# A transformer forward pass in float32 on one core: part of FFN-in by Strassen's scheme, FFN-out in four parts

## Chip, core and metric

The kernel runs on one core of a Trainium2 chip. The metric is the device time of one execution in microseconds (us): the median of three runs of the kernel before is 2635.81 us (2635.48 to 2645.13).

## What is computed

Two stacked blocks of a diffusion-style transformer act on 256 latent tokens (LAT) and 256 context tokens (CTX) of width 1024. The change touches three of four feed-forwards (FFN) of the first block and the modulation vectors. Each FFN normalises its input, modulates it, multiplies by `w_in` (1024 x 5632: a gate and an up half of 2816 columns each), and multiplies the gated product by `w_out` (2816 x 1024):

```
def modulate(h, shift, scale):
    return h * (1.0 + scale) + shift
def swiglu(h, w_in, w_out):
    gate, up = jnp.split(h @ w_in, 2, axis=-1)
    return (jax.nn.silu(gate) * up) @ w_out
...
m_lat = (silu_c @ w_mod[l] + b_mod[l]).reshape(Bsz, N_MOD, 1, D)
m_ctx = (silu_cc @ w_mod[l] + b_mod[l]).reshape(N_MOD, D)
x = x + 0.5 * m_lat[:, 2] * swiglu(modulate(rms_norm(x), m_lat[:, 0], m_lat[:, 1]), ffn_in[l, 0], ffn_out[l, 0])
```

`N_MOD` is 9: each `w_mod[l]` is 1024 x 9216 and gives shift, scale and gate of the three sub-layers of layer l, for the latent and for the context vector. In layer 1 the context is not used behind the mixer.

## The kernel before

Activations lie transposed, features on the 128 partitions: the residual `X` is 128 x 8 x 512, 8 blocks of features by 512 tokens, LAT first. Every product is made of three matmuls (`mm3`, L172 to L174): each float32 operand is split into a high part rounded to float32r and the rest (lo), and hi*hi, hi*lo and lo*hi are summed in PSUM. Weights are loaded by `wload`: SyncE's queue (SP) starts a DMA of 128 x 1024 into a raw tile `wr`, ScalarE (ACT) casts it to `wh` (L156), VectorE (DVE) subtracts to get `wl` (L157). In these stages each of `wr`, `wh` and `wl` has a ring of six tiles.

`ffn` runs FFN-in by units u = 0 to 21, 128 gate and 128 up columns each: two tiles of weights, 2 x 8 x 3 = 48 matmuls of 512 tokens into two banks (`ps_ff`). `hidden` applies Silu on ACT (L536) and multiplies by the up bank on DVE (L537), and splits the result into a `uh` tile, both steps on GpSimd (POOL): the high part (L420) and the rest (L421). The first three units go LAT first, then CTX (`heads`), while the modulated input becomes ready; in the first FFN of the program `opening` does them, interleaved with the first modulation vectors. FFN-in comes in two halves of 12 and 10 units, each followed by FFN-out over those units: for each block m of 8 output blocks, 12 or 10 products of 512 tokens into one bank (`ps_fo`), then `residual` on DVE adds both token halves to `X` (L517). In the second half the last four blocks are computed for LAT first, then for CTX; between the two `tail` starts the norm of the next stage (`ahead`), which so runs under the CTX products.

The modulation vectors not needed yet are computed in small steps between units (`mod_steps`, called by `tick`): for 1024 columns of `w_mod` eight 128 x 1024 tiles are loaded, and DVE accumulates tile times vector into `acc` for LAT and for CTX (L307 for the first tile, L305 for the others); one step is two tiles, four DVE instructions; four steps make 1024 columns and end in matmuls (`ps_mod`). Each FFN has up to 32 steps: the first does 28, the second 32, the third 28.

Tile's scheduler orders each engine's instructions ahead of time; at run time every engine goes through its own queue in order.

## Time and profile before

| | us |
|---|---|
| median of three runs | 2635.81 |
| the profiled execution, its own time | 2637.07 |
| span from its first to its last instruction | 2635.3 |
| PE (TensorE) busy in the span | 2511.4 (95%) |
| DVE busy | 1703.4 (65%) |
| ACT busy | 1006.6 (38%) |
| POOL busy | 668.3 (25%) |

The first FFN ends 426 us from the span's start, the second lies at about 905 to 1307, the third at 1307 to 1697. Matmul ends are modelled: a 512-token matmul is shown as 0.40 us, but the next starts 0.23 us after it; so costs of PE are read from start to start.

### The profile page before, as it was taken

The numbers are of one execution on the slowest core, as the hardware profiler recorded it, in microseconds if no ns is written. First come the engines' busy times: TensorE is split into PE (matmuls) and PEld (weight loads), VectorE is DVE, ScalarE is ACT, GpSimd is POOL, SyncE is SP. The second block draws the span as 40 slices with busy tenths as digits, with TensorE's granted clock in tenths as the row PEclk, the third lists the DMA queues.
The fourth block names the chain that finished last, engine by engine and source line by source line (L and its number), as shares of the span: only waits on it lengthen the run. The fifth ranks groups of instructions, "written<-read, shape, count | busy, mean of one in ns | idle before, by whom it ended". The sixth has DMA issues, their size and how long they took to land.

```text
span 2635.3 us, 46749 instructions
## 1 busy us (share of the span) xinstructions
PE 2511.4 (95%) x19116; PEld 2056.7 (78%) x19116; DVE 1703.4 (65%) x2753; ACT 1006.6 (38%) x1876; POOL 668.3 (25%) x669
## 2 busy tenths in 40 slices
PE   7999999998888999999999999999999999999888
PEld 5777779854776887777887777976999887578775
DVE  4968754558456578776678776487554642855885
ACT  3322224336223432222332122466434643735454
POOL 2420322023443233022242022221413120012321
PEclk9999999989899999999999999999999999999998
DMA  8767543100001556665546665242664331023412
GB/s 262 218 180 217 169 135 109 41 0 1 4 4 51 147 166 182 200 207 153 152 145 191 203 197 152 70 121 73 185 185 134 87 96 41 17 75 99 104 42 64
DMA packets 426502, 321.34 MB, mean 122 GB/s; under 512 B 16784, under 2 KB 400528, under 8 KB 426288
## 3 DMA queue, kind: packets, MB, share of 16 engines
q1 hardware_dynamic: 426288, 318.36, 41.2%
q8 instruction: 150, 2.46, 0.4%
q14 instruction: 64, 0.52, 0.1%
HBM read 317.27 MB, written 1.05 MB: 121 GB/s over the span
## 4 chain that ended last, share of the span: by engine, by line
PE 85%; DVE 8%; ACT 3%; issue 2%; DMA 2%; POOL 0%; DVEq 0%; ACTq 0%; SPq 0%; POOLq 0%
PE ps_ff L172 10%; PE ps_ff L173 10%; PE ps_ff L174 10%; PE ps_pr L172 7%; PE ps_pr L173 7%; PE ps_pr L174 7%; PE ps_fo L172 5%; PE ps_fo L173 5%; PE ps_fo L174 5%; PE ps_s L725 3%; PE ps_o L760 2%; PE ps_w L967 1%; PE ps_ptr L751 1%; PE ps_pt L173 1%; PE ps_pt L174 1%
## 5 line engine op out<-in xcount | busy, mean ns | idle before, releaser
L156 ACT CAST wh<-wr 128x1024 fp32r<-128x1024 f32 (+2 forms) x402 | 417.2, 1043 | 1007.9 <-PE ps_ff L173 407.2
L157 DVE TENSOR_TENSOR wl<-wr,wh 128x1024 fp32r<-128x1024 f32 (+2 forms) x402 | 519.6, 1296 | 402.2 <-ACT wh L156 399.7
L172 PE MATMUL ps_ff<-h,wh 128*128 128x512 f32 (+1 forms) x1232 | 451.9, 367 | 0.5 <-ACT fu L536 0.5
L173 PE MATMUL ps_ff<-h,wh 128*128 128x512 f32 (+1 forms) x1232 | 451.1, 366 | 0.0
L174 PE MATMUL ps_ff<-h,wl 128*128 128x512 f32 (+1 forms) x1232 | 450.5, 366 | 0.6 <-DVE wl L157 0.6
L420 POOL TENSOR_SCALAR uh<-fu 128x512 fp32r<-128x512 f32 (+1 forms) x88 | 169.4, 1925 | 772.9 <-DVE fu L537 772.9
L174 PE MATMUL ps_pr<-h,wl 128*128 128x256 f32 (+2 forms) x920 | 306.5, 335 | 12.3 <-DVE wl L157 12.1
L172 PE MATMUL ps_pr<-h,wh 128*128 128x256 f32 (+2 forms) x920 | 306.4, 338 | 8.9 <-ACT wh L156 6.2
L173 PE MATMUL ps_pr<-h,wh 128*128 128x256 f32 (+2 forms) x920 | 306.6, 335 | 2.0 <-POOL h L457 1.1
L305 DVE SCALAR_TENSOR_TENSOR acc<-wr,csa,acc 128x1024 f32<-128x1024 f32 x224 | 296.3, 1362 | 4.4 <-DMA wr<-in_w_mod_dram 4.4
L172 PE MATMUL ps_fo<-uh,wh 128*128 128x512 f32 (+1 forms) x824 | 278.9, 340 | 0.0
L173 PE MATMUL ps_fo<-uh,wh 128*128 128x512 f32 (+1 forms) x824 | 278.7, 339 | 0.0
L174 PE MATMUL ps_fo<-uh,wl 128*128 128x512 f32 (+1 forms) x824 | 277.7, 338 | 0.0
L172 PEld LDWEIGHTS ps_ff<-h,wh 128*128 128x128 f32 x1232 | 231.6, 188 | 51.7 <-ACT wh L156 6.7
L174 PEld LDWEIGHTS ps_ff<-h,wl 128*128 128x128 f32 x1232 | 231.6, 188 | 42.2 <-DVE wl L157 1.0
L173 PEld LDWEIGHTS ps_ff<-h,wh 128*128 128x128 f32 x1232 | 231.7, 188 | 40.5
L174 PEld LDWEIGHTS ps_pr<-h,wl 128*128 128x128 f32 x920 | 177.6, 193 | 30.3 <-DVE wl L157 14.1
L172 PEld LDWEIGHTS ps_pr<-h,wh 128*128 128x128 f32 x920 | 177.4, 195 | 30.0 <-ACT wh L156 10.1
L173 PEld LDWEIGHTS ps_pr<-h,wh 128*128 128x128 f32 x920 | 177.9, 194 | 19.8 <-POOL h L457 1.6
L172 PEld LDWEIGHTS ps_fo<-uh,wh 128*128 128x128 f32 x824 | 155.0, 188 | 26.7 <-issue 8.4
L173 PEld LDWEIGHTS ps_fo<-uh,wh 128*128 128x128 f32 x824 | 155.0, 188 | 18.7 <-issue 0.8
L174 PEld LDWEIGHTS ps_fo<-uh,wl 128*128 128x128 f32 x824 | 154.9, 188 | 18.2
(628 smaller groups left out, 4207.5 us busy)
## 6 DMA issues: line engine op xcount, KB each, us to landing
wr<-in_ffn_in_dram SPq DMA_DIRECT2D x176, 512.0 KB, 4.6
wr<-in_w_mod_dram SPq DMA_DIRECT2D x144, 512.0 KB, 4.4
wr<-in_ffn_out_dram SPq DMA_DIRECT2D x88, 512.0 KB, 4.4
wr<-in_l_w_in_dram SPq DMA_DIRECT2D x55, 512.0 KB, 3.9
wr<-in_l_w_mod_dram SPq DMA_DIRECT2D x48, 512.0 KB, 4.3
wr<-in_even_w_in_dram SPq DMA_DIRECT2D x21, 512.0 KB, 4.2
wr<-in_l_w_out_dram SPq DMA_DIRECT2D x16, 512.0 KB, 3.6
wr<-in_even_w_out_dram SPq DMA_DIRECT2D x14, 512.0 KB, 4.3
```

What stands on the lines that cost most here:

```text
L156: a = nc.scalar.copy(hi[:, : kt * n], raw)
L157: b = nc.vector.tensor_tensor(lo[:, : kt * n], raw, hi[:, : kt * n].bitcast(F32), ALU.subtract)
L172: mm(ps, a[0], b[0], start=first, stop=False)
L173: mm(ps, a[0], b[1], start=False, stop=False)
L174: self.mm = mm(ps, a[1], b[0], start=False, stop=last)
L305: nc.vector.scalar_tensor_tensor(acc[i], v, cs[:, k, i:i + 1], acc[i], ALU.mult, ALU.add)
L420: nc.gpsimd.tensor_scalar(hi, src, 1.0, None, ALU.mult)
L725: nc.tensor.matmul(s, q(h, q0s[b]), k(h), start=True, stop=True)
L751: nc.tensor.transpose(tr[:, j * 128:(j + 1) * 128], e[:, j * 128:(j + 1) * 128], self.ident)
L760: nc.tensor.matmul(o[64 * par:64 * par + 64, :nq], v(2 * m + par, j), PT[m, par][:, j, :nq], start=j == 0, stop=j == nk - 1, tile_position ...
L967: nc.tensor.matmul(out(rw, b), lhsT[rw, cl], rhs(rw, cl), start=True, stop=True, tile_position=(32 * q, 32 * q))
```

## The change

`ffn2` takes the place of `ffn` in three FFNs (layer 0 both, layer 1 the first). Of its 22 units, the even ones from u = 4 (from u = 6 in the first FFN, `early`) are done by `fast`, the others by `plain` as before. `fast` takes the gate and up tiles, each cut into two halves of the contraction, as a 2 x 2 matrix and the input, cut into two halves of the contraction and LAT and CTX, as another, and forms seven products of 12 matmuls of 256 tokens instead of eight. The sums of input blocks are made once per FFN (`whole`, `T1` to `T4`), those of weights per unit on POOL (`s1` to `s4`, in two more tiles of the `wr` ring), the sums of products on DVE in `e` and `g`. The high part of `uh` is made on ACT, not POOL. FFN-out comes after 6, 6, 6 and 4 units; its weights come in 28 loads, not 22, of the same total, and their `wl` is made on POOL, not DVE; X is updated four times, not twice. Of the last four blocks' CTX products there are now 4 units' worth behind `tail`, not 10. `mod_steps` leaves out the CTX half where it is not used (`one`), and starts with a group of two chunks in the first FFN. A step is taken after every unit from u = 4 (in the first FFN: one after u = 3, two after u = 4) and after every second block of FFN-out.

```diff
+    def wload(self, w, r0, kt, c0, n, eng=None):
         _, raw = self.wraw(w[r0:r0 + kt * 128, c0:c0 + n].rearrange("(k p) n -> p k n", p=128), kt, n)
+        return self.wsplit(raw, n, eng)
...
+    def wsplit(self, raw, n, eng=None):
+        nc, m = self.nc, raw.shape[-1]
         hi, lo = self.wtile("wh", F32R), self.wtile("wl", F32R)
-        a = nc.scalar.copy(hi[:, : kt * n], raw)
-        b = nc.vector.tensor_tensor(lo[:, : kt * n], raw, hi[:, : kt * n].bitcast(F32), ALU.subtract)
+        a = nc.scalar.copy(hi[:, :m], raw)
+        b = (eng or nc.vector).tensor_tensor(lo[:, :m], raw, hi[:, :m].bitcast(F32), ALU.subtract)
...
-        for g in range(start, (nch_all + 3) // 4):
-            nch = min(4, nch_all - 4 * g)
+        n = w.shape[1] // 512
+        at = [4 * start] + list(range(4 * start + 2 if start else 4, n, 4)) + [n]
+        for c0, c1 in zip(at, at[1:]):
+            nch = c1 - c0
...
-                acc = [self.accp.tile([128, 1024], F32, tag=f"acc{i}", name="acc", bufs=1) for i in range(2)]
+                acc = [self.accp.tile([128, 1024], F32, tag=f"acc{i}", name="acc", bufs=1) for i in range(1 if c0 // 2 + h in one else 2)]
...
-                        nc.tensor.matmul(ps[q:q + 32], self.unit[:, h], acc[i][:, c * 512:c * 512 + 512], start=h == 0, stop=2 * h + 2 == nch, tile_position=(0, q))
+                        nc.tensor.matmul(ps[q:q + 32], self.unit[:, h], acc[i % len(acc)][:, c * 512:c * 512 + 512], start=h == 0, stop=2 * h + 2 == nch, tile_position=(0, q))
...
+    def ffn2(self, l, f, name, j, segs, tail):
...
+            UH = lambda dt, nm: p.tile([128, 2, 512], dt, tag="uh", name=nm, bufs=6)
+            fu = lambda: p.tile([128, 512], F32, tag="fu", name="fu", bufs=1)
+            def keep(u):
+                uh = UH(F32R, "uh")
+                self.split(uh[:, 0], uh[:, 1], u, "a", "p")
+                hid.append(uh)
+            def hidden(ps):
+                u = fu()
+                nc.scalar.activation(u, ps[0], AF.Silu)
+                nc.vector.tensor_tensor(u, u, ps[1], ALU.mult)
+                keep(u)
...
+            block = lambda t, k, s: t[:, 4 * k:4 * k + 4, s]
+            TT = p.tile([128, 4, 2, 4, 256], F32R, name="TT")
+            def whole(k, s, eng, tag):
+                t = p.tile([128, 1024], F32, tag=tag, name="tf", bufs=6 if tag == "uh" else 1).rearrange("p (k n) -> p k n", n=256)
+                eng.tensor_tensor(t, block(hi, k, s).bitcast(F32), block(lo, k, s).bitcast(F32), ALU.add)
+                return t
+            b11, b21 = whole(0, LAT, nc.gpsimd, "uh"), whole(1, LAT, nc.gpsimd, "uh")
+            b12, b22 = whole(0, CTX, nc.vector, "acc0"), whole(1, CTX, nc.gpsimd, "acc1")
+            nc.vector.tensor_tensor(b11, b12, b11, ALU.subtract)
+            nc.gpsimd.tensor_tensor(b12, b22, b12, ALU.subtract)
+            nc.vector.tensor_tensor(b22, b22, b11, ALU.subtract)
+            nc.gpsimd.tensor_tensor(b21, b21, b22, ALU.subtract)
+            T2, T1, T3, T4 = ((TT[:, i, 0], TT[:, i, 1]) for i in range(4))
+            self.split(*T2, b22, "a", "v")
+            self.split(*T1, b11, "a", "v")
+            self.split(*T3, b12, "a", "v")
+            self.split(*T4, b21, "a", "p")
+            B11, B21, B22 = ((block(hi, k, s), block(lo, k, s)) for k, s in ((0, LAT), (1, LAT), (1, CTX)))
...
+            def fast(u):
+                G, U = (self.wraw(w_in[:, o + u * 128:o + u * 128 + 128].rearrange("(k p) n -> p k n", p=128), KD, 128)[1] for o in (0, FF))
+                a11, a12, a21, a22 = G[:, 0:512], G[:, 512:1024], U[:, 0:512], U[:, 512:1024]
+                S12, S34 = self.wtile("wr", F32), self.wtile("wr", F32)
+                s1, s2, s3, s4 = S12[:, 0:512], S12[:, 512:1024], S34[:, 0:512], S34[:, 512:1024]
+                gh, gl = self.wsplit(G, 128)
+                nc.gpsimd.tensor_tensor(s1, a21, a22, ALU.add)
+                nc.gpsimd.tensor_tensor(s2, s1, a11, ALU.subtract)
+                h12, l12 = self.wsplit(S12, 128)
+                nc.gpsimd.tensor_tensor(s3, a11, a21, ALU.subtract)
+                nc.gpsimd.tensor_tensor(s4, a12, s2, ALU.subtract)
+                h34, l34 = self.wsplit(S34, 128)
+                h22, l22 = self.wsplit(a22, 128)
+                e = p.tile([128, 2, 256], F32, tag="fe", name="fe", bufs=1)
+                g = fu()
+                sub, add, mul = ALU.subtract, ALU.add, ALU.mult
+                def product(h, l, k0, b):
+                    ps = self.psa.tile([128, 512], F32, tag="a", name="ps_ff")[:, 0:256]
+                    for k in range(4):
+                        self.mm3(ps, [h[:, k0 + k], l[:, k0 + k]], [b[0][:, k], b[1][:, k]], k == 0, k == 3)
+                    return ps
+                tt = nc.vector.tensor_tensor
+                p1 = product(gh, gl, 0, B11)
+                nc.scalar.copy(e[:, 0], p1)
+                p2 = product(gh, gl, 4, B21)
+                tt(g[:, LAT], e[:, 0], p2, add)
+                p6 = product(h12, l12, 4, T2)
+                tt(e[:, 0], e[:, 0], p6, add)
+                p5 = product(h12, l12, 0, T1)
+                nc.scalar.copy(e[:, 1], p5)
+                p7 = product(h34, l34, 0, T3)
+                tt(g[:, CTX], e[:, 0], e[:, 1], add)
+                tt(e[:, 0], e[:, 0], p7, add)
+                p3 = product(h34, l34, 4, B22)
+                tt(g[:, CTX], g[:, CTX], p3, add)
+                nc.scalar.activation(g, g, AF.Silu)
+                tt(e[:, 1], e[:, 0], e[:, 1], add)
+                p4 = product(h22, l22, 0, T4)
+                tt(e[:, 0], e[:, 0], p4, add)
+                tt(g, g, e.rearrange("p a n -> p (a n)"), mul)
+                keep(g)
+            early = (l, f) == (0, 0)
+            steps = 32
+            for part, pairs in enumerate((range(0, 3), range(3, 6), range(6, 9), range(9, 11))):
+                end = part == 3
+                if part:
+                    hid.clear()
+                u0 = pairs[0] * 2
+                for u in range(u0, u0 + 2 * len(pairs)):
+                    if len(hid) <= u - u0:
+                        (plain if u % 2 or early and u < 6 else fast)(u)
+                    if u > 3 or early and u == 3:
+                        steps -= self.tick(1 + (early and u == 4), steps)
+                nk = len(hid)
+                rest = 4 if end else 0
+                wide = 8 // nk
+                side = {}
+                def blocks(m):
+                    if m % wide == 0:
+                        side[0] = self.wload(w_out, u0 * 128, nk, m * 128, wide * 128, nc.gpsimd)
...
+                for m in range(8 - rest):
+                    b = blocks(m)
+                    product(*b, slice(0, 512))
+                    self.residual(b[1], m, name, j + 2, segs)
+                    if m % 2:
+                        steps -= self.tick(1, steps)
...
-        self.fill += [m0, self.mod_steps("1", self.i["w_mod"][1], fx),
-                      self.mod_steps("s0", self.i["l0_w_mod_2"], fs, "l0_norm"), self.mod_steps("s1", self.i["l1_w_mod_2"], fs, "l1_norm")]
+        self.fill += [m0, self.mod_steps("1", self.i["w_mod"][1], fx, one=(5, 6, 7, 8)),
+                      self.mod_steps("s0", self.i["l0_w_mod_2"], fs, "l0_norm"), self.mod_steps("s1", self.i["l1_w_mod_2"], fs, "l1_norm", one=(2,))]
...
-            self.ffn(0, 0, "0", 0, segs, 2, tail=ahead)
+            self.ffn2(0, 0, "0", 0, segs, ahead)
-            self.ffn(0, 1, "0", 6, segs, 2, tail=ahead)
+            self.ffn2(0, 1, "0", 6, segs, ahead)
         if upto == 3:
             return self.dump()
         if frm < 4:
-            self.ffn(1, 0, "1", 0, segs, 2, tail=ahead)
+            self.ffn2(1, 0, "1", 0, segs, ahead)
```

## Rows read from the trace of the kernel before

**Rows 1.** The page: busy times, and the chain that ended last by engine.

```profile
PE 2511.4 (95%) x19116; PEld 2056.7 (78%) x19116; DVE 1703.4 (65%) x2753; ACT 1006.6 (38%) x1876; POOL 668.3 (25%) x669
...
PE 85%; DVE 8%; ACT 3%; issue 2%; DMA 2%; POOL 0%; DVEq 0%; ACTq 0%; SPq 0%; POOLq 0%
```

**Rows 2.** Windows of the three FFNs: length, busy per engine, clock, DMA share, GB/s.

```profile
74.00:426.00 352.00, 349.80 (x1660) 281.53 (x1659) 246.48 (x247) 90.75 (x119) 96.80 (x60) 1.00 0.58 174
955.00:1307.00 352.00, 351.75 (x1667) 281.81 (x1665) 253.39 (x250) 84.98 (x111) 90.13 (x56) 1.00 0.60 179
1345.00:1697.00 352.00, 350.76 (x1671) 282.79 (x1669) 239.97 (x243) 86.23 (x113) 85.91 (x57) 1.00 0.56 168
```

**Rows 3.** Timeline of PE, 512 tokens: the first and last of 12 matmuls.

```profile
177.27 0.40 PE L172 MATMUL ps_ff<-h,wh 128*128 128x512 f32 x1
...
179.84 0.40 PE L174 MATMUL ps_fo<-uh,wl 128*128 128x512 f32 x1
```

**Rows 4.** Timeline of PE, 256 tokens (fourth FFN): the first and last of 36.

```profile
1959.83 0.28 PE L172 MATMUL ps_ff<-h,wh 128*128 128x256 f32 x1
...
1963.97 0.28 PE L174 MATMUL ps_ff<-h,wl 128*128 128x256 f32 x1
```

**Rows 5.** The page's costliest groups: a weight load of `ps_ff`.

```profile
L172 PEld LDWEIGHTS ps_ff<-h,wh 128*128 128x128 f32 x1232 | 231.6, 188 | 51.7 <-ACT wh L156 6.7 <-issue 3.4 <-ACT fu L536 0.9
```

**Rows 6.** Timeline of PE in the second FFN: matmuls of the modulation steps.

```profile
1197.59 1.07 PE L315 MATMUL ps_mod<-acc,unit 128*32 128x512 f32 x8
...
1203.82 0.95 PE L324 MATMUL ps_mod<-c_small,gm 128*128 128x8 f32 x8
```

**Rows 7.** DVE groups by form, 1059 to 1129 us (FFN-out): busy, mean ns.

```profile
L305 DVE SCALAR_TENSOR_TENSOR acc<-wr,csa,acc 128x1024 f32<-128x1024 f32 x27 | 33.4, 1275 | 0.0
L157 DVE TENSOR_TENSOR wl<-wr,wh 128x1024 fp32r<-128x1024 f32 x13 | 15.8, 1218 | 11.8 <-ACT wh L156 11.7
L517 DVE SCALAR_TENSOR_TENSOR X<-ps_fo,M,X 128x256 f32<-128x256 f32 x14 | 6.1, 476 | 2.6 <-PE ps_fo L174 2.6
L307 DVE TENSOR_SCALAR acc<-wr,csa 128x1024 f32<-128x1024 f32 x4 | 2.8, 750 | 0.2
```

**Rows 8.** DVE groups by form, whole run: the product in `hidden`, both widths.

```profile
L537 DVE TENSOR_TENSOR fu<-fu,ps_ff 128x512 f32<-128x512 f32 x57 | 38.8, 681 | 92.0 <-PE ps_ff L174 91.9
L537 DVE TENSOR_TENSOR fu<-fu,ps_ff 128x256 f32<-128x256 f32 x20 | 8.4, 421 | 12.5 <-PE ps_ff L174 12.5
```

**Rows 9.** Timeline of DVE in the first FFN: four in a row, then one.

```profile
113.56 4.86 DVE L305 SCALAR_TENSOR_TENSOR acc<-wr,csa,acc 128x1024 f32<-128x1024 f32 x4
...
84.36 2.34 DVE L157 TENSOR_TENSOR wl<-wr,wh 128x1024 fp32r<-128x1024 f32 x1
```

**Rows 10.** Timeline of POOL at the same place as the last.

```profile
84.33 1.29 POOL L421 TENSOR_TENSOR uh<-fu,uh 128x512 fp32r<-128x512 f32 x1
```

**Rows 11.** Timeline of DVE and of POOL in the mixer, at one time.

```profile
662.53 1.29 DVE L924 TENSOR_TENSOR GM<-ps_g,c_em_mask 128x512 f32<-128x512 f32 x2 [0.83 <-PE ps_g L921]
...
662.98 1.05 POOL L953 TENSOR_TENSOR AS<-ARw,EC 128x512 f32<-128x512 f32 x1
```

**Rows 12.** Timelines at the end of the second FFN, then a window.

```profile
1288.80 0.74 POOL L391 TENSOR_TENSOR nacc<-nacc,nsq 128x256 f32<-128x256 f32 x1 [2.81 <-ACT nsq L389]
...
1291.21 0.48 DVE L517 SCALAR_TENSOR_TENSOR X<-ps_fo,M,X 128x256 f32<-128x256 f32 x1 [3.07 <-PE ps_fo L174]
...
1300.73 2.15 DVE L449 SCALAR_TENSOR_TENSOR nt<-X,M,nacc 128x256 f32<-128x256 f32 x4
...
1308.76 0.36 PE L172 MATMUL ps_pr<-h,wh 128*128 128x256 f32 x1 [1.66 <-DVE X L517]
...
1309.00:1312.40 3.40, 3.40 (x18) 3.40 (x18) 3.40 (x5) 1.46 (x4) 2.77 (x1) 0.52 0.19 52
```

**Rows 13.** Timelines of DVE and POOL at the first turn to FFN-out.

```profile
182.06 0.68 DVE L537 TENSOR_TENSOR fu<-fu,ps_ff 128x512 f32<-128x512 f32 x1
...
185.31 1.29 POOL L421 TENSOR_TENSOR uh<-fu,uh 128x512 fp32r<-128x512 f32 x1
```

More of the change, by code (lines that the diff above doesn't have):

```diff
@@ L307, in mod_steps @@
                             a = nc.vector.tensor_scalar(acc[i], v, cs[:, k, i:i + 1], None, ALU.mult)
-                            if start and (g, h) == (start, 0):
+                            if start and (c0, h) == (at[0], 0):
                                 self.order(a, self.gate[1])
@@ L331, in mod_steps @@
                     b[:, sl].rearrange("p (c s) -> p s c", s=4), ALU.add)
-            for j in (2 * g, 2 * g + 1):
+            for j in range(c0 // 2, c1 // 2):
                 if j in fixes:
@@ L350, in tick @@
     def tick(self, n=1, left=99):
-        for _ in range(n):
+        for i in range(n):
             if not self.open and left < 8:
-                return
+                return i
             left -= 1
@@ L595, in ffn, with plain, product @@
                         left -= ticks
+                last = [blocks(m) for m in range(8 - rest, 8)]
+                for s, i in segs if rest else ():
+                    for b in last:
+                        product(*b, s)
+                        self.residual(b[1], b[0], name, j + 2, [(s, i)])
+                    if s == LAT:
+                        tail()
+            assert not self.open
+    def ffn2(self, l, f, name, j, segs, tail):
+        nc, tc = self.nc, self.tc
+        w_in, w_out = self.i["ffn_in"][l, f], self.i["ffn_out"][l, f]
+        with ExitStack() as es:
+            p = es.enter_context(tc.tile_pool(name=f"ffn{l}{f}", bufs=1))
+            mod = self.modulate(name, j)
+            self.psum(es, 6, 1, 1)
+            self.accp = p
+            hid = []
+            UH = lambda dt, nm: p.tile([128, 2, 512], dt, tag="uh", name=nm, bufs=6)
[9 more added lines that the diff above has]
+                keep(u)
+            first = []
+            done = lambda m, q: first.append(q) or len(first) % 2 or hidden(first[-2:])
+            items = [(w_in, o + u * 128, 0, done) for u in range(3) for o in (0, FF)]
+            if (l, f) == (0, 0):
+                hi, lo = self.opening(mod, items, segs)
+            else:
+                tiles = self.fetch(items)
+                hi, lo = self.modulated(mod, segs)
+                self.heads((hi, lo), tiles, segs)
+            block = lambda t, k, s: t[:, 4 * k:4 * k + 4, s]
[16 more added lines that the diff above has]
+            B11, B21, B22 = ((block(hi, k, s), block(lo, k, s)) for k, s in ((0, LAT), (1, LAT), (1, CTX)))
+            def plain(u):
+                ps = []
+                for o in (0, FF):
+                    w = self.wload(w_in, 0, KD, o + u * 128, 128)
+                    q = self.psa.tile([128, 512], F32, tag="a", name="ps_ff")
+                    for k in range(KD):
+                        self.mm3(q, [w[0][:, k], w[1][:, k]], [hi[:, k], lo[:, k]], k == 0, k == KD - 1)
+                    ps.append(q)
+                hidden(ps)
+            def fast(u):
[58 more added lines that the diff above has]
+                        side[0] = self.wload(w_out, u0 * 128, nk, m * 128, wide * 128, nc.gpsimd)
+                    c = slice(m % wide * 128, m % wide * 128 + 128)
+                    q = self.psa.tile([128, 512], F32, tag="a", name="ps_fo")
+                    return m, q, [tuple(x[:, k, c] for x in side[0]) for k in range(nk)]
+                def product(m, q, w, toks):
+                    for k in range(nk):
+                        self.mm3(q[:, toks], w[k], [hid[k][:, 0, toks], hid[k][:, 1, toks]], k == 0, k == nk - 1)
+                for m in range(8 - rest):
[4 more added lines that the diff above has]
+                        steps -= self.tick(1, steps)
```

16 lines of the change are left out of this document (7 added, 9 removed).

## The prediction

> **What bounds the kernel now.** I read the page first: TensorE (PE) is busy 95% of the span and 85% of the chain that ended last [rows 1]. Then the windows of the three FFNs that change: PE is busy for 349.8 to 351.8 of 352 us at full clock, DVE for 240 to 253, POOL for 86 to 97, ACT for 85 to 91, and the DMA engines for 0.56 to 0.60 [rows 2]. The reader is to see that in these stages only columns taken from PE give time back, and that PE has no slack in which work moved to others could be late. The profiled execution took 2637.07 us, 1.26 above the median of 2635.81; sums are made against the former, and 1.3 is taken off at the end.
>
> **What PE gains.** Twelve matmuls of 512 tokens stand 2.57 us apart from first to last, 0.2336 us each [rows 3]; 36 of 256 tokens 4.14 us, 0.1183 each [rows 4]. A plain unit costs 48 x 0.2336 = 11.2 us, a fast one 84 x 0.1183 = 9.9. There are 8 fast units in the first FFN and 9 in each of the others: 26 x 1.27 = **33 us**. FFN-out keeps its matmuls.
>
> Every matmul loads its own weights, and a load takes 0.188 us [rows 5], longer than the 0.118 step of a 256-token matmul, so the loads already run under other matmuls. The Trainium skill, page "TensorE: Matmul & The Clock Gate", Part 3, The mechanism, says that a weight load overlaps running matmuls only when its row group differs; all these use all rows. By that rule a fast unit would cost 84 x (0.118 + 0.188) = 25.7 us against 48 x (0.234 + 0.188) = 20.3, and the change would lose 26 x 5.4 = 140 us. The rows contradict it, and it gets no chance.
>
> **What DVE and POOL pay.** DVE instructions in a row overlap by 0.08 us: four L305 last 4.86 [rows 9], a step of 1.20 each against a mean of 1.275 [rows 7]. So I take 1.14 for L157, 0.40 for L517, 0.67 for L307 [rows 7], 0.60 and 0.34 for L537 at 512 and 256 tokens [rows 8], these two also for the new sums of those widths, which the trace doesn't show. Four modulation steps are 14 L305 and 2 L307, 18.1 us, 4.53 a step; half where one vector is left out.
>
> The decisive rows are those where DVE and POOL meet. An L157 that starts with POOL's L421 of 1.29 us takes 2.34 instead of 1.22: DVE stood 1.12 [rows 9, 10]. A DVE product that reads one operand from PSUM keeps its time beside a POOL instruction of two inputs, which keeps its 1.05 too [rows 11]. So two-input work from SBUF on the two engines doesn't add up side by side; it queues. A POOL instruction of 512 columns that writes float32 takes 1.05 [rows 11], one that writes float32r 1.29 [rows 10], and one of 256 columns 0.74 [rows 12]. From these I estimate 1.85 us for 768 columns, 2.4 for 1024, and 1.7 for 1024 in float32, and at 1.12/1.29 = 87% a stall of DVE of 0.91 per `s` sum, 1.12 per L421, 1.6 per `wl` of FFN-out, and 9.4 in all for the six POOL instructions of `whole` and T4.
>
> The Trainium skill, page "SBUF — State Buffer", Who interferes with whom, says that a two-input DVE instruction and a GpSimd instruction that reads SBUF exclude each other for the whole instruction. By that rule the stall is 1.29, not 1.12, and the forecast would be about 10 us later; I keep the row.
>
> Now **one pair of units** (plain and fast) with two full steps. PE: 11.2 + 9.9, and the matmuls of two steps, at most 0.4 each (eight of 1.07 in all per four steps, eight of 0.95 per eight) [rows 6]: 21.9 us. DVE from SBUF: plain 2 x 1.14; fast 3 x 1.14 + 0.60 for the half tile, 2 x 0.34 + 0.60; steps 9.1: 16.7. DVE from PSUM: 0.60 + 5 x 0.34 = 2.3. POOL's stall: 4 x 0.91 + 2 x 1.12 = 5.9. If POOL always works while DVE reads PSUM, DVE needs 22.6; if never, 24.9. Before, two units took PE 23.2 and DVE 4 x 1.14 + 1.2 + 9.1 + 2.2 = 17.1. So DVE with POOL becomes the limit, by 0.7 to 3.0 us a pair. I take 23.6, **1.7 over**: POOL's instructions are often pending when DVE turns to PSUM. With half steps DVE needs 19.1, and PE stays the limit.
>
> **FFN-out** of six units: PE 48 x 3 x 0.2336 = 33.6 and 1.6 for four steps, 35.2. DVE: 18.1 in steps, 16 x 0.40 = 6.4 for four-part residuals (PSUM), stalls of 8 x 1.6 = 12.9: 31.0 to 37.4, since moving `wl` to POOL takes 8 x 0.86 off DVE and gives 12.9 back as stall. I take 34: within PE's time.
>
> **The setup** of the input's sums is 6 x 1.14 on DVE and 9.4 of stall. In the first FFN it meets units 3 to 5 with four steps: 6.8 + 18.1 + 6.8 + 3.4 + 9.4 and 1.8 from PSUM, 44.5 to 46.3 against PE's 35.2, so 10 over. In the other two it can run under the CTX half of `heads`; I leave 2 each.
>
> Half steps are the second FFN's last twelve and the third's first four and last four; counted through, six pairs of units with full steps stand in each FFN ahead of its last part, which is light. **Excess**: first FFN 10 + 6 x 1.7 = 20; second 2 + 6 x 1.7, less 2.8 that a pair with half steps gives back, 9; third 2 + 6 x 1.7 = 12; 41 us. Against it stands DVE's lead: six `wl` tiles make one pair, so at the start of a stretch its tiles can be some 10 us ahead. That would leave 10, 0 and 2. But a part's last L537 stands at the end of what DVE has queued: at the first turn it ended at 182.7, some 4 us after FFN-in's last matmul, and L421 at 186.6 [rows 3, 13]; that cost nothing because eleven units' products, 7.7 us, come before its own in the first block of FFN-out. Now five do, 3.5 us. What DVE is behind comes out there. I take **22 us**, between 12 with the whole lead and 41 without.
>
> **The ends of the FFNs.** Between the last LAT and the end of CTX PE had 4 x 10 x 3 x 0.1183 = 14.2 us; it will have 5.7. From the last LAT residual to the first modulated tile it took 9.5 us (1291.2 to 1300.7), and PE began 8 us later, at 1308.8, and then for 3.4 us was granted 0.52 of the clock, nearly all of it the lower of its two levels, 1.2 GHz [rows 12]. The chain's own pieces (a square, two small matmuls, a root, a copy) are shorter than 5.7; what stretched it were casts, L157 and matmuls queued between. So 0 to 5.5 per FFN; I take **5** in all.
>
> **The rest at nothing.** ACT takes over the high part of `uh` and 1.5 casts per fast unit more, some 3 us of a pair, at a busy share of a quarter [rows 2]; if ACT fell behind, POOL's `s` sums would wait for nothing, but casts of the next unit would. SP issues six more loads per FFN and gives two `wr` tiles per fast unit to S12 and S34; DMA is at 0.6 [rows 2], but with a load's wait uncovered each would cost PE up to its landing. On POOL's queue `s1` to `s4` stand behind the last unit's L421, which waits for L537; behind `s4` wait the cast and L157 of the last two products. The new wait of PE is for them, covered by a whole plain unit, 11 us. Regrouping the modulation chunks changes no count.
>
> **Sum**: 2637.1 - 33 + 22 + 5 = 2631; on the median, **2630 us**.
>
> **Rivals.** First, **the lead holds**: excess at its floor of 0.7 a pair, all but 4 us absorbed, 2 us at the ends: -33 + 6, 2609. For it: PE idles 0.2 to 2.2 us in each window and DVE about 100 [rows 2], so the order of the queues leaves room. Against it: the pair's sum above uses that room up. Second, on the other side, **the shared path is the limit**: no earlier lead helps and each part's excess comes out at its turn to FFN-out: 41 us at the middle price, 81 at the upper ones (24.9 and 37.4). The ends cost 10, and at each of 12 turns half of the 2.5 us by which a chain of 6 us (4 to L537's end, a cast, L421) outlasts its 3.5 of cover, 15. That gives 2637 - 33 + 41 + 10 + 15 = 2670, without the turns 2655; I take 2662, with 2710 as the upper end. It decides from the point where DVE and POOL together need over 23 us a pair. If waits then bring PE to its lower clock [rows 12], it is more. Third, that fast units do not come to 9.9 us because products of 12 matmuls wait for banks: part of the second, no case of its own.
>
> **Chances.** Forecast 0.42 (2618 to 2648), first rival 0.26 (2604 to 2618), second 0.32 (2649 to 2710). Half a per cent, 13 us, is about what can be told from no change here. Faster than 2622.6: the first rival's 0.26 and 0.10 of the forecast's, 0.36. Slower than 2649: 0.32. Within: 0.32. For eight in ten I leave some 0.08 below 2608 and 0.1 above 2676.
>
> **What will show it.** Right: `ps_ff` at 256 tokens steps by 0.118 in these FFNs; DVE busy over 95% in the windows of FFN-in with full steps; L157 and L305 of over 2 us beside POOL's L421 and `s` sums; PE's idle time in these FFNs some 25 us, ended by DVE (`wl`, or `uh` at the turns to FFN-out), most in the first FFN. Wrong: PE busy all through (first rival), or idle over 50 us or at the lower clock (second); a wait for DMA or ACT would show that I set them to nothing wrongly.

## The result, and the profile after

The changed kernel takes 2779.91 us (2778.77 to 2781.82) against 2635.91 for the kernel before: **1.053 times as long** (95% interval 1.050 to 1.056). The forecast was 2630. The page of its profiled execution (busy times, then the chain by engine):

```profile
PE 2543.0 (92%) x19836; PEld 2107.5 (76%) x19836; DVE 1907.3 (69%) x2995; ACT 1120.8 (40%) x2076; POOL 965.5 (35%) x809
...
PE 58%; DVE 22%; issue 8%; DMA 5%; ACT 4%; POOL 3%; SPq 0%; DVEq 0%; ACTq 0%; POOLq 0%
```

Against [rows 1], DVE and POOL are busy 204 and 297 us longer and PE's share of the chain has fallen from 85% to 58%. The three feed-forwards, from the first unit behind `heads` to the last product (columns as in [rows 2]):

```profile
73.00:489.00 416.00, 363.45 (x1874) 298.25 (x1874) 324.99 (x329) 122.64 (x171) 183.81 (x99) 0.94 0.50 152
1034.00:1421.00 387.00, 356.36 (x1917) 296.26 (x1916) 317.21 (x325) 119.45 (x168) 176.64 (x96) 0.96 0.57 172
1465.00:1849.00 384.00, 355.71 (x1918) 297.30 (x1916) 302.67 (x321) 119.07 (x168) 182.96 (x97) 0.96 0.54 162
```

Read from the timeline to a tenth, these spans are 415.6, 387.1 and 383.8 us, 1186.5 together; before they were 350.2, 351.6 and 350.2, 1052.0. So 134.5 us of the loss lie inside the three FFNs and some 10 outside them. PE's matmuls should have taken 33 less: 168 us have to be explained. DVE is busy for 78 to 82% of these spans, though PE is idle in them for 28 to 52 us (length less busy time) and is granted less than the full clock. Three FFN-in stretches of six units:

```profile
166.00:262.00 96.00, 77.65 (x422) 65.78 (x421) 81.08 (x85) 26.66 (x38) 36.03 (x18) 0.89 0.57 173
297.00:386.00 89.00, 72.39 (x417) 61.15 (x417) 82.61 (x79) 23.80 (x33) 35.55 (x17) 0.94 0.61 190
1111.00:1200.00 89.00, 74.51 (x420) 63.56 (x419) 86.95 (x81) 24.65 (x34) 37.33 (x17) 0.90 0.66 202
```

The forecast's own prices give PE 65.7 us for three pairs of units. DVE is busy 84, 93 and 98% of the time: in the worst stretch it is not full. What a wait costs shows on PE's timeline in the second FFN:

```profile
1262.32 0.28 PE L176 MATMUL ps_ff<-TT,wh 128*128 128x256 f32 x1
...
1263.62 0.28 PE L178 MATMUL ps_ff<-TT,wl 128*128 128x256 f32 x1
1263.83 2.07 PE L320 MATMUL ps_mod<-acc,unit 128*32 128x512 f32 x8
1268.79 0.38 PE L176 MATMUL ps_ff<-TT,wh 128*128 128x256 f32 x1 [2.89 <-DVE fe L718]
...
1270.51 0.41 PE L177 MATMUL ps_ff<-TT,wh 128*128 128x256 f32 x1
1270.73 0.41 PE L178 MATMUL ps_ff<-TT,wl 128*128 128x256 f32 x1
1273.28 0.58 PE L176 MATMUL ps_ff<-TT,wh 128*128 128x256 f32 x1 [2.14 <-ACT fe L703]
```

The first two rows are the ends of one product: 11 steps in 1.30 us, 0.118 each, as costed [rows 4]. Then PE waits for a sum on DVE, falls to half its clock (0.22 a step; 0.50 is granted from 1271 on, 1.2 GHz) and waits again, for the copy of a first product. The third reading is ACT's timeline at one turn from a fast to a plain unit, and POOL's at the same time:

```profile
199.34 1.04 ACT L160 CAST wh<-wr 128x1024 fp32r<-128x1024 f32 x1 [1.94 <-DMA wr<-in_ffn_in_dram]
208.77 1.05 ACT L160 CAST wh<-wr 128x1024 fp32r<-128x1024 f32 x1 [8.39 <-POOL wr L685]
209.72 0.58 ACT L325 COPY gm<-ps_mod 128x512 f32<-128x512 f32 x1
210.20 0.62 ACT L422 CAST uh<-fu 128x512 fp32r<-128x512 f32 x1
...
212.67 0.60 ACT L633 ACTIVATE fu<-ps_ff 128x512 f32<-128x512 f32 x1 [1.30 <-POOL uh L427]
```

```profile
201.40 3.46 POOL L684 TENSOR_TENSOR wr<-wr 128x512 f32<-128x512 f32 x1 [13.94 <-DVE fe L718]
...
207.03 1.71 POOL L685 TENSOR_TENSOR wr<-wr 128x512 f32<-128x512 f32 x1
208.82 1.60 POOL L688 TENSOR_TENSOR wr<-wr 128x512 f32<-128x512 f32 x1
210.90 1.74 POOL L427 TENSOR_TENSOR uh<-fu,uh 128x512 fp32r<-128x512 f32 x1 [0.48 <-ACT uh L422]
```

The fast unit's last product stood ready in `fu` at 207.6 (L719 on DVE, 205.86 and 1.75). Its cast came at 210.2, because ACT's queue first waited 8.4 us for POOL's second weight sum and cast it; its low part on POOL ended at 212.64; only then could the plain unit's Silu (L633) write `fu`, of which there is **one** buffer where the kernel before has two. The chain begins before POOL: its first sum, at 201.40, reads an up tile that landed at 201.19, because SP's queue had issued the load only at 197.23. Loads wait for a free tile of the `wr` ring, and the weight sums S12 and S34 take two of its six; no run changes that ring by itself.

### The profile page after: what moved, and what is told of

Its sections match the earlier page's. It is cut to its first block, busy times and chain, and to the rows that moved or that the text cites. A ratio compares the mean times of both kernels' runs of the same rounds, so it can differ in the third digit from the quotient of the medians.

```text
span 2779.0 us, 49084 instructions
## 1 busy us (share of the span) xinstructions
PE 2543.0 (92%) x19836; PEld 2107.5 (76%) x19836; DVE 1907.3 (69%) x2995; ACT 1120.8 (40%) x2076; POOL 965.5 (35%) x809
## 4 chain that ended last, share of the span: by engine, by line
PE 58%; DVE 22%; issue 8%; DMA 5%; ACT 4%; POOL 3%; SPq 0%; DVEq 0%; ACTq 0%; POOLq 0%
DVE acc L310 7%; PE ps_pr L176 6%; PE ps_pr L177 6%; PE ps_pr L178 6%; PE ps_ff L176 4%; PE ps_ff L177 4%; PE ps_ff L178 4%; DVE wl L161 4%; PE ps_fo L176 4%; PE ps_fo L177 3%; PE ps_fo L178 3%; PE ps_s L885 3%; DMA wr<-in_ffn_in_dram 2%; PE ps_o L920 2%; PE ps_w L1127 1%
## 5 line engine op out<-in xcount | busy, mean ns | idle before, releaser
L160 ACT CAST wh<-wr 128x1024 fp32r<-128x1024 f32 (+2 forms) x472 | 461.9, 987 | 887.3 <-PE ps_ff L177 205.0
L161 DVE TENSOR_TENSOR wl<-wr,wh 128x1024 fp32r<-128x1024 f32 (+3 forms) x388 | 499.0, 1292 | 307.9 <-ACT wh L160 306.5
L176 PE MATMUL ps_ff<-h,wh 128*128 128x256 f32 (+1 forms) x1128 | 384.1, 341 | 53.9 <-ACT wh L160 15.7
L177 PE MATMUL ps_ff<-h,wh 128*128 128x256 f32 (+1 forms) x1128 | 379.9, 337 | 0.0
L178 PE MATMUL ps_ff<-h,wl 128*128 128x256 f32 (+1 forms) x1128 | 379.0, 336 | 0.0
L310 DVE SCALAR_TENSOR_TENSOR acc<-wr,csa,acc 128x1024 f32<-128x1024 f32 x196 | 327.0, 1697 | 29.7 <-DMA wr<-in_w_mod_dram 29.3
L176 PEld LDWEIGHTS ps_ff<-h,wh 128*128 128x128 f32 x1128 | 216.6, 192 | 88.7 <-ACT wh L160 18.5
L176 PE MATMUL ps_fo<-uh,wh 128*128 128x512 f32 (+1 forms) x752 | 262.8, 359 | 9.3 <-ACT uh L422 5.2
L177 PE MATMUL ps_fo<-uh,wh 128*128 128x512 f32 (+1 forms) x752 | 268.8, 359 | 2.3 <-POOL uh L427 2.3
L161 POOL TENSOR_TENSOR wl<-wr,wh 128x768 fp32r<-128x768 f32 (+1 forms) x84 | 192.3, 2296 | 222.9 <-ACT wh L160 198.4
L177 PEld LDWEIGHTS ps_ff<-h,wh 128*128 128x128 f32 x1128 | 216.9, 192 | 22.5
L427 POOL TENSOR_TENSOR uh<-fu,uh 128x512 fp32r<-128x512 f32 (+1 forms) x88 | 138.9, 1578 | 166.8 <-ACT uh L422 161.3
L176 PEld LDWEIGHTS ps_fo<-uh,wh 128*128 128x128 f32 x752 | 142.4, 190 | 39.7 <-ACT uh L422 6.0
L177 PEld LDWEIGHTS ps_fo<-uh,wh 128*128 128x128 f32 x752 | 142.9, 190 | 28.9 <-POOL uh L427 4.2
```

The lines of the kernel that those rows point to most:

```text
L160: a = nc.scalar.copy(hi[:, :m], raw)
L161: b = (eng or nc.vector).tensor_tensor(lo[:, :m], raw, hi[:, :m].bitcast(F32), ALU.subtract)
L176: mm(ps, a[0], b[0], start=first, stop=False)
L177: mm(ps, a[0], b[1], start=False, stop=False)
L178: self.mm = mm(ps, a[1], b[0], start=False, stop=last)
L310: nc.vector.scalar_tensor_tensor(acc[i], v, cs[:, k, i:i + 1], acc[i], ALU.mult, ALU.add)
```

## Experiments

Times are single runs unless a count is given; "before" is the kernel before, timed beside it on the same chip. The ten runs of e17 lie 15 us apart (2644.2 to 2659.6), so smaller differences of whole times show nothing by themselves. The last column is the sum of the three FFN spans as defined above, each from one profile; how far it scatters for one kernel was not measured, and differences of a few us are not read.

| run | us | before | FFNs |
|---|---|---|---|
| kernel before / changed kernel | 2635.9 / 2779.9 | | 1052.0 / 1186.5 |
| e1 steps cut to 8 columns | 2639.7 | 2633.3 | 1052.1 |
| e2 POOL's share on DVE | 2704.1 | 2633.3 | 1111.8 |
| e3 all units plain, no input sums | 2644.0 | 2633.3 | 1053.0 |
| e4 no weight sums | 2730.5 | 2633.3 | 1126.7 |
| e5 FFN-out's steps ordered | 2786.0 | 2643.5 | 1188.1 |
| e6 and FFN-out's `wl` ordered | 2811.7 | 2643.5 | 1210.1 |
| e7 setup's sums elsewhere | 2776.6 | 2643.5 | 1172.6 |
| e8 e2, e5 and e7 together | 2762.7 | 2643.5 | 1172.1 |
| e9 two products in a bank | 2850.9 | 2635.3 | 1235.3 |
| e10 e9, e2 and e7 | 2809.5 | 2635.3 | 1206.1 |
| e11 two `e`, two `fu`, no T4 | 2716.2 | 2635.3 | 1119.7 |
| e12 steps spread | 2794.5 | 2635.3 | 1176.7 |
| e13 two `e` | 2786.4 | 2637.4 | 1188.6 |
| e14 two `e`, two `fu` | 2730.2 | 2637.4 | 1131.1 |
| e15 e14, e2 and e7 | 2663.1 | 2637.4 | 1082.0 |
| e16 e15 and two products in a bank | 2679.0 | 2637.4 | 1080.2 |
| e17 e15 with 14 fast units | 2651.8 (10 runs) | 2640.9 | 1060.3 |
| e18 e15 with steps cut to 8 columns | 2656.4 | 2640.9 | 1031.9 |

### What the loss needs: load, engines, fast units

e1:

```diff
-nc.vector.scalar_tensor_tensor(acc[i], v, cs[:, k, i:i + 1], acc[i], ...)
+nc.vector.scalar_tensor_tensor(acc[i][:, 0:8], v[:, 0:8], cs[:, k, i:i + 1], acc[i][:, 0:8], ...)
```

> The changed kernel with the modulation accumulations behind the first of each group cut from 1024 to 8 columns (the modulation vectors are therefore not computed); every load, every wait and the order of steps stay. It takes some 85% of the steps' time off DVE. Theory A (DVE and POOL are one path, and FFN-in holds more of its work than PE has time for): PE becomes the limit, 2600 to 2645 us. Theory B (the loss is in fast's own chain: four sums on POOL, two tiles of the ring, one e and one fu buffer, banks of PSUM): that chain is all there, 2720 us or more.

e2 (and the same for `s2`, `s3`, `s4`):

```diff
-nc.gpsimd.tensor_tensor(s1, a21, a22, ALU.add)
+nc.vector.tensor_tensor(s1, a21, a22, ALU.add)
-self.split(uh[:, 0], uh[:, 1], u, "a", "p")
+self.split(uh[:, 0], uh[:, 1], u, "a", "v")
-side[0] = self.wload(w_out, u0 * 128, nk, m * 128, wide * 128, nc.gpsimd)
+side[0] = self.wload(w_out, u0 * 128, nk, m * 128, wide * 128)
```

> The changed kernel with POOL's share of the three feed-forwards given to DVE: the four weight sums of a fast unit, the low part of uh, and wl of FFN-out. Theory A: POOL's instructions were not free, each held DVE up for longer than DVE itself needs for the same work (0.6 against some 0.9 to 1.1 us for 512 columns, 0.87 against 1.6 for 768), so the kernel gets faster, 2670 to 2730 us. If POOL is a second engine beside DVE, some 170 us of work more on DVE make it slower, over 2850 us.

e3:

```diff
-(plain if u % 2 or early and u < 6 else fast)(u)
+plain(u)
```

> The changed kernel with every unit plain and without the input sums: what is left of the change is FFN-out in four parts, its wl on POOL, the high part of uh on ACT and the place of the steps. PE's gain of 33 us is gone. Theory A: per part, DVE with POOL's stall needs about 70 to 73 us in FFN-in where PE has 70, so 2650 to 2690 us. Theory B (the loss comes with the fast units' chain alone): 2636 to 2650 us. If FFN-out in four parts is itself what costs: 2720 us or more.

e4:

```diff
-S12, S34 = self.wtile("wr", F32), self.wtile("wr", F32)
+S12, S34 = G, U
-nc.gpsimd.tensor_tensor(s1, a21, a22, ALU.add)
...
```

> The changed kernel without the four weight sums of a fast unit on POOL: casts and products read the loaded gate and up tiles in their place (the result of a fast unit is therefore not the unit's), and the two ring tiles are not taken. Theory A: 26 x 4 POOL instructions of 0.9 to 1.9 us go off the shared path, 95 to 200 us, until PE is the limit: 2630 to 2690 us. If the sums run hidden beside DVE and the ring was not short, 2760 us or more.

Without the steps' load 134 of the 168 us are back; the other 33 stay though DVE has little to do, and e18 below shows that 20 of them go with one `fu` buffer, POOL's share and the setup. With all units plain the FFNs take 1053.0: **four-part FFN-out, its `wl` on POOL, the shorter ends and one `fu` buffer cost nothing beside plain units**; the loss comes with the fast units. Without the weight sums 60 us come back in the FFNs, but e4 frees their two ring tiles too, so the 60 are not POOL's alone. And POOL's share on DVE brings 75. The page of that kernel:

```profile
PE 2517.1 (93%) x19836; PEld 2086.6 (77%) x19836; DVE 1890.6 (70%) x3249; ACT 1119.2 (41%) x2076; POOL 467.1 (17%) x555
```

DVE does 254 instructions more than in the changed kernel, POOL's busy time is 498 us shorter, and DVE is busy 17 us *less*. The accumulations in one FFN-in stretch, first in the changed kernel, then without POOL beside them (by form, busy, mean ns):

```profile
L310 DVE SCALAR_TENSOR_TENSOR acc<-wr,csa,acc 128x1024 f32<-128x1024 f32 x29 | 45.4, 1593 | 6.5 <-DMA wr<-in_w_mod_dram 6.5
```

```profile
L310 DVE SCALAR_TENSOR_TENSOR acc<-wr,csa,acc 128x1024 f32<-128x1024 f32 x35 | 43.8, 1276 | 4.2 <-DMA wr<-in_w_mod_dram 4.2
```

The kinds of instruction that were moved, on DVE in that stretch (a weight sum, FFN-out's `wl`, the low part of `uh`):

```profile
L688 DVE TENSOR_TENSOR wr<-wr 128x512 f32<-128x512 f32 x3 | 2.0, 679 | 0.0
L161 DVE TENSOR_TENSOR wl<-wr,wh 128x768 fp32r<-128x768 f32 x5 | 4.7, 948 | 0.0
L427 DVE TENSOR_TENSOR uh<-fu,uh 128x512 fp32r<-128x512 f32 x4 | 2.7, 682 | 0.0
```

At these means 104 sums, 84 `wl` and 66 low parts are some 195 us of DVE's own work. As its busy time fell by 17, POOL's instructions must have held it up for about 210 (an estimate from these rows). Having these instructions on POOL bought DVE no time at all. (The Trainium skill, page "Perfetto Trace Analysis", section "Optimizing Scalar/DVE Operations", says that the two share a read port, so that moving work from one to the other might not help; these rows agree.)

### A theory that fell: where the steps stand

In the changed kernel's queue many of the steps that the text puts into FFN-out stand in FFN-in, in runs of up to five accumulations. I took that for the cause.

e5 (the order is only for DVE's queue; nothing waits more):

```diff
+if self.pin is not None:
+    self.order(a, self.pin)      # a: the accumulation
...
 if m % 2:
+    self.pin = self.last_res     # the block's residual
     steps -= self.tick(1, steps)
+    self.pin = None
```

> The changed kernel with one thing ordered: the modulation steps that the program text puts between the blocks of FFN-out may not stand ahead of those blocks' residuals in DVE's queue. In the changed kernel's queue 41, 32 and 33 accumulations stand in the first three FFN-in stretches of the first FFN, 16, 37 and 16 in the second, 12, 32 and 28 in the third; so ordered it is 28, 26, 25; 8, 25, 22; 4, 26, 26. Same work, same engines. Theory A (the unit prices were right, but the scheduler put FFN-out's steps into FFN-in): 57 accumulations of 1.2 to 1.7 us leave stretches in which DVE is the limit for ones where it idles: 2685 to 2715 us. If the loss is within fast's own chain, or the total of DVE's work: 2765 us or more.

e6 adds the same for FFN-out's `wl` on POOL, behind the last low part of `uh`:

```diff
+if eng is not None and self.lastlo is not None:
+    self.order(b, self.lastlo)
```

> As the run with the steps ordered, and FFN-out's wl on POOL, from its second block on, ordered behind the last low part of uh (five of eight stood in FFN-in). Theory A: 5 x 1.6 us of stall leave each FFN-in stretch with steps, some 50 to 70 us, of which the new wait at the turn to FFN-out (POOL's first wl some 6 us behind the last unit) takes 2 to 4 us at each of nine turns: 20 to 40 us faster than the run without it. If POOL's wl costs DVE nothing in FFN-in, it is slower than that run by the waits, 20 to 40 us.

e12 cuts the steps into pairs of accumulations, each behind one sum, product or residual:

```diff
-if k % 2 and k < KD - 1:
+if k < KD - 1:
     yield
...
 tt(e[:, 0], e[:, 0], p6, add)
+some(1)                          # one pair, ordered behind this sum
...
 tt(g[:, CTX], g[:, CTX], p3, add)
+some(1)
```

> The changed kernel with the modulation steps cut into pairs of accumulations and each pair ordered behind one sum, product or residual of DVE's queue: at most two accumulations stand between two of fast's sums, where runs of up to five stand now; FFN-in and FFN-out get the shares that they got when only FFN-out's steps were ordered. Work and engines are the same. Theory C: PE's waits behind runs of steps go, 2690 to 2740 us. Theory A: as that run, 2775 to 2790 us.

e5 and e6 missed theory A, e12 theory C: 1188, 1210 and 1177 in the FFNs, against 1186.5. In e5 the first stretch takes 91 us in place of 96, with DVE busy for 78 of them; the fourth and the fifth of the six take 8 us more each. The order moved less than was put down: in the traces the six stretches of six units hold 186 accumulations in the changed kernel and 165 in e5. What e12 gained in the FFNs is 10 us. They were run beside one `fu` buffer, which, as shown below, sets the pace there; what the order is worth with two was not tried.

### The setup in the first FFN

In the changed kernel PE waits there once for 13.8 us for a cast, while SP's queue waits for a ring tile that the first accumulation has to free:

```profile
PE ps_ff L176 <- ACT wh L160: 15.7, 2, 13.8
...
SPq L148 <- DVE acc L312: 26.4, 1, 26.4
```

e7:

```diff
-b12, b22 = whole(0, CTX, nc.vector, "acc0"), whole(1, CTX, nc.gpsimd, "acc1")
+b12, b22 = whole(0, CTX, nc.vector, "wh"), whole(1, CTX, nc.gpsimd, "wl")   # slots of the rings
```

> The changed kernel with two of the setup's four sums in slots of the wh and wl rings, not in the accumulators' place. In the first FFN PE waited 14 us for a weight tile behind raw tiles of w_mod that waited for the first accumulation, which waited for the accumulators. Theory A: that wait goes, 2762 to 2770 us. If the setup's work on DVE and POOL itself is what the units wait for there, 2778 us or more.

The wait is gone and the first FFN takes 399.8 for 415.6 us. The whole time shows it only against the kernel before timed beside it (+133, not +144). e8 puts e2, e5 and e7 together:

> The three together: POOL's share given to DVE, the steps of FFN-out ordered behind its residuals, two sums of the setup in slots of the rings. Theory A: the FFN-in stretches of 90, 86, 82 us come down to 67 to 72, the first FFN loses its 13 us wait: 2620 to 2650 us. If the loss left after giving POOL's share to DVE is in fast's chain of single buffers and banks, 2685 us or more.

It should have been the best and is 60 us slower in the FFNs than e2 alone. Ordering the steps takes back most of what the other two gain there; why it costs so much beside them and nothing in e5 was not settled.

### Banks, and the buffers of `e` and `fu`

e9 and e10:

```diff
-ps = self.psa.tile([128, 512], F32, tag="a", name="ps_ff")[:, 0:256]
+if not half:
+    q = self.psa.tile([128, 512], F32, tag="a", name="ps_ff")
+    half.extend((q[:, 256:512], q[:, 0:256]))
+ps = half.pop()
```

> The changed kernel with two products of a fast unit in the two halves of one bank: four banks for a fast unit in place of seven. Theory C (formed after ordering the steps brought nothing): six banks covered three plain units, 33 us, before; of a fast unit they cover six products, 8.5 us, and DVE, at work nearly all the time in which PE is late, comes to a product's sum only behind a run of steps and wl. With twice the cover 40 to 90 us come back: 2690 to 2740 us. Theory A (the time that DVE and POOL need together): 2770 us or more. If the one e buffer is what a product waits for, 2765 us or more.

> As the last, and POOL's share given to DVE (which gave 76 us by itself), and two sums of the setup in slots of the rings (some 12). Theory C: 2630 to 2670 us. Theory A, with DVE's own need all that is left: 2685 to 2695 us. If cover and POOL's stall are the same loss counted twice: 2675 to 2695 us.

Both became slower than the changed kernel, by a wait of their own: in this form a product waits for the reader of the one that shares its bank. PE's longest wait of one stretch in e9 (L717 reads the other half of the bank that PE is to write):

```profile
PE ps_ff L176 <- DVE fe L717: 16.8, 2, 9.1
```

So they say nothing on banks; e16 does.

e11:

```diff
-e = p.tile([128, 2, 256], F32, tag="fe", name="fe", bufs=1)
+e = p.tile([128, 2, 256], F32, tag="fe", name="fe", bufs=2)
-fu = lambda: p.tile([128, 512], F32, tag="fu", name="fu", bufs=1)
+fu = lambda: p.tile([128, 512], F32, tag="fu", name="fu", bufs=2)
```

> The changed kernel with two buffers for e and two for g, in place of one each; the room comes from T4, which is left out with its three instructions (the seventh product reads T1, so a fast unit's result is not the unit's). If a fast unit's first copy and sum wait for the last unit's e and g: 40 us or more faster, below 2740 us. Theory C and theory A: 2760 to 2780 us, of which up to 10 faster by the setup's shorter chain in each FFN.

64 us faster, in a kernel without T4. e13 and e14 leave nothing out; e13 is the first pair of lines, e14 adds the second:

```diff
-e = p.tile([128, 2, 256], F32, tag="fe", name="fe", bufs=1)
+e0, e1 = (self.normp.tile([128, 256], F32, tag="nt", name="fe", bufs=4) for _ in range(2))
...
-fu = lambda: p.tile([128, 512], F32, tag="fu", name="fu", bufs=1)
+fu = lambda: p.tile([128, 512], F32, tag="fu", name="fu", bufs=2)
```

> The changed kernel with two sets of buffers for e (1 KB each, in the four temporary tiles of the norm, idle here) and still one for g and for the hidden product; nothing is left out. The last product with e comes in two instructions of 256 columns. Theory D1 (a fast unit's first copy waits for the last unit's e): 2715 to 2740 us. Theory D2 (the one fu buffer, which passes from the plain unit's hidden product to the fast unit's g only when POOL has made the low part from it, is what holds the chain): 2765 to 2785 us.

> As the last, with the place of e used for a second fu buffer, so that the hidden products have two, as in the kernel before. D2: 2710 to 2740 us. D1: no faster than the last run. If the gain of the run with two buffers of each came from leaving out T4: 2765 us or more in both.

It is theory D2: two `e` give nothing (+2 in the FFNs), the second `fu` gives **57 us**. What waited for `fu`, in the waits from the first to the third FFN (sum, times, longest), in the changed kernel and in e14:

```profile
ACT wh L160 <- POOL wr L685: 101.5, 16, 8.7
ACT fu L633 <- POOL uh L427: 39.5, 24, 4.7
```

```profile
ACT wh L160 <- POOL wr L685: 164.3, 23, 10.2
...
ACT fu L633 <- POOL uh L427: 3.4, 4, 1.7
```

The Silu no longer waits for POOL's low part. ACT still waits for the weight sums, now even longer.

> As the last, with POOL's share (weight sums, low part of uh, FFN-out's wl) given to DVE and two sums of the setup in slots of the rings. If buffers and POOL's stall are separate losses: 64 and 76 and some 12 us off 2780, 2625 to 2650 us. If they are one loss, POOL's late low part holding fu: 2685 to 2705 us.

> As the last, with two products of 256 columns in each bank, and both halves' matmuls ahead of the sums that read them (when they shared banks but not in that order, a product waited for the sum of the other half: PE waited 17 us at two such places in one FFN-in stretch). Theory C (six banks cover too little of DVE's queue): 15 to 40 us faster than the last run. If banks no longer matter with two buffers, within 8 us of it.

(In e16 both halves' matmuls stand ahead of the sums that read them.) e15 takes 49 us more off the FFNs than e14. Beside one `fu` buffer POOL's share and the setup's place gave 75 and 14, so some 40 us of these were the same waiting as the buffer's; the whole time, 2663, lies between the two ranges put down. Two products in a bank change the FFNs by 2 us: in the FFNs banks do not matter beside two buffers. The whole time of e16 is 16 us longer than e15's, outside the FFNs.

### What is left

e17 and e18, on e15:

```diff
-(plain if u % 2 or early and u < 6 else fast)(u)
+(plain if u % 4 or early and u < 6 else fast)(u)
```

> The kernel with two fu buffers, POOL's share on DVE and the setup's sums in the rings, with fast only for every fourth unit: 14 fast units in place of 26, the others plain. PE's gain is 14 x 1.27 = 18 us against the run with all units plain (8 to 11 us over the kernel before). If a loss comes only where DVE's work in a stretch exceeds PE's (from a point on): nearly all of the 18 us stays, 2625 to 2640 us. If every fast unit brings its loss with it: between the all-plain run and the run with 26, 2645 to 2660 us.

> The kernel with two fu buffers, POOL's share on DVE and the setup's sums in the rings, and 26 fast units, with the modulation accumulations behind the first of each group cut to 8 columns (the modulation vectors are therefore not computed). If what is left of the loss, some 60 us over 2603, is DVE's load: 2605 to 2620 us. If it lies in PE's own matmuls or in the setup and the ends of the FFNs: 2635 us or more.

e17 is 1.004 times the kernel before (1.0022 to 1.0058) and lies in the range put down for a loss that every fast unit brings with it. It is 11 us over the kernel before; with no fast unit (e3) it was 11 over, with 26 (e15) 26 over. In the FFNs 14 units cost 7 us more than none and 26 cost 29 more, so the loss does not grow evenly either; e3, though, has one `fu` buffer and POOL's share, and is not quite of this series. 14 units bring about what they cost. No version beat the kernel before.

e18's whole time looks like a miss, but its FFNs are what was expected:

```profile
72.00:419.00 347.00, 341.13 (x1873) 286.52 (x1872) 222.84 (x410) 121.50 (x171) 24.82 (x17) 0.99 0.58 178
987.00:1330.00 343.00, 339.75 (x1922) 286.80 (x1920) 220.60 (x417) 121.36 (x172) 19.19 (x14) 1.00 0.64 197
1371.00:1714.00 343.00, 339.48 (x1920) 287.34 (x1919) 215.01 (x409) 120.35 (x170) 18.39 (x15) 1.00 0.61 184
151.00:216.00 65.00, 65.00 (x411) 57.44 (x411) 44.41 (x95) 24.01 (x35) 0.00 (x0) 1.00 0.72 222
```

1031.9 us, 20 less than before and 13 over the ideal 1019 (1052 less the 33 of fewer matmuls); the last row is a stretch of three pairs with PE busy throughout. Its whole time is longer by the mixer between the first two FFNs, which the change doesn't touch: it took 568 us in this run, at a lower granted clock (last section).

## Why the prediction was wrong, point by point

The 168 us against the forecast's 27 (22 for DVE and POOL, 5 for the ends): **57** by the second `fu` buffer (e13 to e14), **49** by POOL's share and the setup's place (e14 to e15), **50** by the steps' load on DVE beside fast units (e15 to e18), 13 left over the ideal, less the 2 by which e13 is slower. The shares hold for this order of runs; e1 and e2 show that in another they would be of other sizes, since each takes away part of the same waiting. From the changed kernel to e18 the windows above lose 99 us of PE's idle time and 55 of its busy time: the matmuls are the same, so about a third of this difference goes with the lower clock that PE was granted (0.94 to 0.96 against 0.99 to 1.00).

**PE's gain: right.** The step is 0.118; three pairs take PE 65.6 to 66.6 us in e18 where the steps give 65.7; PE's busy time per FFN falls from 350 to 340, 11.4 at most were promised. (The rule of the Trainium skill, page "TensorE: Matmul & The Clock Gate", Part 3, The mechanism, that a weight load overlaps running matmuls only when its row group differs, by which fast units would have been dearer, is contradicted by these steps once more; the same section also has a load to the background weight buffer pulled ahead of running matmuls, which the forecast passed over.)

**The step that failed: "The rest at nothing".** That paragraph weighs ACT's time, SP's ring and POOL's queue, but not the line of the diff that gives `fu` one buffer, while the kernel before had two; the prediction never mentions it. And what it says of ACT is the wrong way round: it asked what happens if ACT falls behind, and ACT at 30% does not. ACT's *queue* stands still: the high part of `uh`, moved from POOL to ACT, is queued behind the cast of S12, which waits for POOL's sums, 8.4 us in the rows above and 101.5 in all. Then the low part waits, then `fu`, then the next unit's Silu, then PE's banks. With one buffer in place of two this chain set PE's pace: 57 us. That the buffer is what cost them is shown by e13 and e14; what the cast's move to ACT adds is read from the rows alone, since no run moved it back. The prediction's own sign for this error, a wait of PE for ACT, came: 13.8 us for a cast, in the setup's case below.

**The step that was mis-sized: DVE and POOL, 22 us.** With two `fu` buffers (e14), so without that chain, six FFN-in stretches of six units take 70.5 to 80.6 us, 75.5 in the mean against 65.7: 10 over, where the term has 5. In all, this term, the ends and the rest measure 112 us (49, 50 and 13) in place of 27. The price of POOL's work was not too low: for the 254 instructions of e2 the forecast's stalls add up to some 300 us (104 x 0.91, 66 x 1.12, 84 x 1.6), where the estimate from e2 is about 210; that DVE would need less for them by itself stood in its own prices and was not drawn on. What failed is the term's form. It compares busy times in a pair, 23.6 against 21.9, as if DVE were a pipe that is full or not. In the changed kernel's stretch of 96 us PE was late by some 20 us, an estimate from the starts of its matmuls; DVE was at work for nearly all of them, some 12 on accumulations, and yet idle for some 13 us in the rest of the stretch. e15 has a stretch of 67 us with DVE at 61 and PE never late, so a nearly full DVE need not cost anything:

```profile
266.00:333.00 67.00, 67.00 (x423) 58.18 (x422) 60.61 (x80) 24.36 (x34) 0.00 (x0) 1.00 0.63 193
```

What decides between such a stretch and one of 78 us in the same kernel is open: not banks alone (e16), and the place of the steps was tried only beside one `fu` buffer (e5, e6, e12).

**The setup**: 10 us in the first FFN were costed, for its work. 16 were measured (e7), and they were a wait of the DMA queue for ring tiles, not work: the accumulators lent to the setup held up the first accumulation, this the raw tiles, and these the next weights. The prediction had looked at SP's ring for S12 and S34 alone.

**The ends and FFN-out**: 5 us and 34 against 35.2; e3 measures 1 us for all of FFN-out in four parts, beside plain units. Right there, and if anything too careful.

**The rivals.** The second, "the shared path is the limit", had the sign and half the cause, but at 2662, and 2710 at its upper end, 70 us too little. Its marks came true: PE idle for more than 50 us (52, 31 and 28 in the three FFNs), in part at the lower clock. The forecast's mark did not: DVE over 95% in FFN-in. It was 84 to 98%, and a bound engine that is idle a sixth of the time while the other one waits for it is the mark of a chain of queues, which none of the cases was. The third, banks, was no case of its own there, and e16 finds nothing in it.

## What to carry to other kernels

Before summing busy times, go through a diff for every buffer count and every instruction that changes its queue, and ask of each what has to happen on all engines before the buffer is free again: here that loop ran over DVE, ACT and POOL, and it cost more than the arithmetic saved. Give GpSimd two-input work from SBUF only where DVE has none at that time; test it by taking it back, since DVE's busy time can fall. When an engine's busy share is below full while the next one waits for it, sums of busy times do not tell a chain from load: take each away by itself, as here, where less load (e1) and one more buffer (e14) both gave time back.

## What the runs showed of the hardware that was not expected

DVE took over 254 instructions from POOL and was busy 17 us less, as shown above: the stall that these instructions brought DVE from POOL, about 210 us, was no shorter than DVE's own time for the same work, some 195 us (both estimates from e2's rows).

The same mixer code, between the first and the second FFN, took 568 us in e18 and 536 in e1. In its rwkv part PE was about as busy in both, DMA stood still, and the granted clock was 0.66 in one window of 100 us of e18 and 0.89 in the like one of e1:

```profile
620.00:720.00 100.00, 91.71 (x1143) 54.70 (x1142) 43.85 (x139) 33.08 (x92) 21.84 (x36) 0.66 0.01 1
```

```profile
635.00:735.00 100.00, 87.65 (x1796) 61.44 (x1795) 58.84 (x174) 38.86 (x110) 31.44 (x50) 0.89 0.01 2
```

What made the clock lower in this run is not known. 32 us hang on this, more than some of the effects sought; that is why the FFNs were compared by their own spans.
